# A recalibrated list scheduler in a two-layer diffusion backbone: other latencies, other engine preferences, the first modulation loaded ahead

## The chip, the cores and the metric

The kernel runs on one core of a Trainium2 chip. The metric is the device time of one execution in microseconds (us); lower is better. TensorE (PE) multiplies matrices, VectorE (DVE), ScalarE (ACT) and GpSimd (POOL) work element by element, and SyncE (SP) issues the loads and stores. Each of the five runs its own instructions strictly in the order in which they were issued, and waits on semaphores for what the others produce.

## What is computed

A latent stream `x` of 512 tokens with 1024 features passes two layers, each a modulated RMSNorm, a mixer, a gate and a gated residual; a final RMSNorm follows. Everything is float32. The reference, cut to what matters:

```python
# layer 0
xn = modulate(rms_norm(x, g), shift(c), scale(c))        # adaln: silu(c) @ ada_w + b
cn = modulate(rms_norm(ctx, g), shift(c_ctx), scale(c_ctx))
h = xn @ w_in                                            # conv input, q, k, v and the gate
u = a_val * sigmoid(a_gate); u = depthwise_conv(u, 31 taps)
a = silu(layer_norm(u))
att = latent_window_attention(rope(q), rope(k), v, kc, vc, sink)   # blocks of 128, window and 256 context keys
y = (concat([a, att]) * silu(h_gate)) @ w_out
x = x + gt * y
# layer 1
h = modulate(rms_norm(x, g1), sh1, sc1) @ od_w_in         # bg, cg, u, z of 2048 each
x = x + gt1 * ((bg * depthwise_conv(cg * u, 3 taps)) * silu(z)) @ od_w_out
return rms_norm(x, final_g)
```

## The kernel before, in words

The host only rearranges the weights. In the kernel, activations lie with features on partitions, 1024 features in eight tiles of 128 x 512 (`k` = 0 to 7). Each float32 operand is split into a rounded high part (suffix `h`, a copy on ACT) and the rest (suffix `l`, a subtraction); a product is three matmuls, hi x hi, hi x lo and lo x hi (`mm3`).

The program records every operation first (class `Plan`; so all rows have line L481, the place where they are issued) and then orders them: `schedule()` plays the five engines with modelled durations (`cost`), a delay between producer and consumer (`LAG`, `HOP`), a model of the load queue, and priorities. A priority is the place in the program plus a bias that a stream carries (`CONV_BIAS`, `GATE_BIAS`, `LN_BIAS`, `OUT_BIAS` and so on). An operation issued through `F` may run on DVE or POOL: it goes where the model ends it first, after `SHY` has added a handicap in nanoseconds to DVE. `LOOK` and `HELD` say how long an engine may be kept free for a more urgent operation and for the turn of an SBUF port that the model lets DVE and POOL take one after the other. What comes out is one fixed order for each engine.

The stages, with the names that rows show. *Start:* `cols`, `ccol`, `crow` (the conditioning), four token tiles `xt` and two context tiles `ct` are loaded; `crow` goes through a matmul and Silu into `silb`; ACT squares the tokens (`xt0q`), their factor `xt0r` comes from POOL, and DVE scales them. *Modulation of tile k* (`modulation`): weights `adas` give the shift (`pmod`, 8 small products with `ccol`), `ada` times `silb` gives the scales `mod`, both end in `mab`. *Projection:* for each k the tokens are turned (`tp`, in one PSUM bank "cv"), modulated by ACT, split into `xh` and `xl`, and multiplied with `ws` for keys, queries and values (`pk`, `pq`, `sv`; `pkc` for the context). *Attention:* four groups of four blocks; scores `s`, their maximum by a reduction on DVE (two in each block), `p` by Exp on ACT with the negative maximum `nm`, transposes `pt`, split into `th` and `tl`, product `po`. Between them stand the products of the convolution's input (`ag`, `av`), later queries (`pq`) and gates (`pg`). The 31-tap convolution of a channel tile runs as a chain of `cv` instructions on DVE (30, after one on ACT), for tiles 0 and 5 as `pr`/`cp` on ACT and POOL. *Gate and LayerNorm:* eight gate products `pgc` with weights `wgc0` to `wgc7`, and over the eight convolved tiles `u` a LayerNorm: `lnsum` adds up seven tiles, `lnm` is their mean by a matmul, `u<-u,lnmean` subtracts it, `lnsq` adds the squares, `lnq` sums them by matmuls, `lnb` and `lnr` spread mean and factor. *Output:* `pya` with `woa` (the attention's half, needs no LayerNorm), then `pya`/`pyb` with `woc` (the convolution's half, needs `z0` to `z7`). *Between the layers:* `x` plus the gated output in two halves of columns (hf), squares `sq`, their sum `st`, `xm`, `yh`, `yl`. The modulation of layer 1 comes from `as` and `ac` products, eight each, through one buffer "ad". *Layer 1:* products `pcg`, `pu`, `pbg`, `pz` for 16 tiles, a mixer on DVE, then `f`.

## Time and profile before

| | us |
|---|---|
| median of 3 runs (lowest, highest) | 1005.02 (1001.16, 1007.85) |
| the profiled execution | 1005.3 |
| its span | 1003.5 |
| PE busy in the span | 970.0 (97%) |
| DVE busy | 605.8 (60%) |
| ACT busy | 487.7 (49%) |
| POOL busy | 409.3 (41%) |

The profile's span begins with the first instruction and ends with the last; some 1.8 us lie around it. The share of busy time is a mean over stages with different limits. A row of a timeline gives a start, a duration and, in brackets, how long the engine stood idle before it and what ended that idle time. The profile also lists the clock that was granted to TensorE (1.00 is 2.4 GHz, half of it 1.2 GHz).

### The profile page before, as it was taken

Reading aid. Unit: us, or ns where it says so; the run is one execution under the profiler, and the core shown is the slowest. Engines: PE = TensorE matmul, PEld = TensorE weight load, DVE = VectorE, ACT = ScalarE, POOL = GpSimd, SP = SyncE. Lnnn points to the kernel's source line nnn. Section 1 sums busy time; section 2 is a strip of 40 time slices with the busy share of each in tenths; the row PEclk is TensorE's granted clock in tenths of the full one; section 3 lists DMA queues with packets and bytes.
Section 4 is the critical chain, followed back from the end, with each engine's and each line's share of the span. In section 5 each row is a group of like instructions: output and inputs, shape, how many; then the busy total and the mean of one; then the engine's idle time right before and its main releaser. Section 6 shows DMA issues by size and latency. Waiting matters only on the chain.

```text
span 1003.5 us, 13484 instructions
## 1 busy us (share of the span) xinstructions
PE 970.0 (97%) x4996; PEld 806.4 (80%) x4996; DVE 605.8 (60%) x982; ACT 487.7 (49%) x923; POOL 409.3 (41%) x368
## 2 busy tenths in 40 slices
PE   8989999999999999699999999999999999999997
PEld 5988777778778778578898988888888888888886
DVE  4635887987888889767316666544444444542443
ACT  6647779776887864434425323223323333222332
POOL 4615787666878868878866200000000000000111
PEclk9989999999999999989999999999999999999999
DMA  8632111112121516243154235332332322322222
GB/s 328 212 141 64 64 43 42 43 42 93 56 84 58 175 63 220 96 156 118 63 189 165 89 126 193 101 105 88 101 104 86 105 89 101 105 84 91 98 85 85
DMA packets 31750, 109.11 MB, mean 109 GB/s; under 512 B 3650, under 2 KB 3778, under 8 KB 31684
## 3 DMA queue, kind: packets, MB, share of 16 engines
q1 hardware_dynamic: 31684, 108.25, 32.2%
q8 instruction: 39, 0.64, 0.3%
q14 instruction: 27, 0.22, 0.1%
HBM read 106.14 MB, written 2.10 MB: 108 GB/s over the span
## 4 chain that ended last, share of the span: by engine, by line
PE 77%; DVE 7%; POOL 4%; DMA 4%; ACT 4%; issue 2%; SPq 0%; POOLq 0%; ACTq 0%; DVEq 0%
PE pbg L481 9%; PE pcg L481 9%; PE pz L481 9%; PE pu L481 9%; PE f L481 8%; PE pya L481 6%; PE pq L481 3%; DVE cv L481 3%; PE s L481 3%; PE po L481 3%; PE ag L481 3%; PE pt L481 3%; PE av L481 2%; PE pgc L481 2%; PE sv L481 2%
## 5 line engine op out<-in xcount | busy, mean ns | idle before, releaser
L481 POOL TENSOR_TENSOR x1t<-x1t,fg 128x512 f32<-128x512 f32 x4 | 6.8, 1722 | 392.5 <-ACT fy L481 392.5
L481 DVE SCALAR_TENSOR_TENSOR cv<-u,cols,cv 128x512 f32<-128x512 f32 x180 | 135.4, 752 | 14.6 <-ACT cv L481 10.6
L481 POOL TENSOR_TENSOR cp<-cp,pr 128x512 f32<-128x512 f32 x60 | 78.9, 1315 | 3.6 <-ACT pr L481 1.6
L481 DVE TENSOR_TENSOR tl<-pt,th 128x512 fp32r<-128x512 f32 x72 | 48.1, 689 | 22.6 <-ACT th L481 21.1
L481 PE MATMUL pt<-ident,p 128*128 128x128 f32 x288 | 49.4, 277 | 3.6 <-ACT p L481 3.2
L481 ACT ACTIVATE th<-pt 128x512 fp32r<-128x512 f32 x72 | 41.0, 595 | 20.5 <-PE pt L481 19.6
L481 ACT ACTIVATE p<-s,nm 128x512 f32<-128x512 f32 (+1 forms) x64 | 46.8, 739 | 7.3 <-DVE nm L481 6.9
L481 PEld LDWEIGHTS pt<-ident,p 128*128 128x128 f32 x288 | 35.7, 140 | 17.1 <-ACT p L481 9.9
L481 DVE TENSOR_REDUCE s<-s 128x2 f32<-128x1024 f32 (+1 forms) x32 | 43.5, 1359 | 4.1 <-PE s L481 3.7
L481 ACT ACTIVATE pr<-u,cols 128x512 f32<-128x512 f32 x60 | 41.4, 718 | 5.5 <-POOL cp L481 3.9
L481 PE MATMUL po<-th,vv 128*128 128x512 f32 x72 | 31.0, 431 | 0.6 <-ACT th L481 0.5
L481 PE MATMUL po<-tl,vv 128*128 128x512 f32 x72 | 31.0, 430 | 0.2 <-DVE tl L481 0.2
L481 DVE TENSOR_TENSOR ya<-ya,sz 128x512 f32<-128x512 f32 x16 | 11.1, 692 | 31.0 <-ACT sz L481 30.9
L481 DVE SCALAR_TENSOR_TENSOR ac<-ac,silc 128x1024 f32<-128x1024 f32 x6 | 9.6, 1594 | 29.2 <-DMA ac<-in_ada_dram 29.2
L481 ACT ACTIVATE sz<-pz 128x512 f32<-128x512 f32 x16 | 9.6, 597 | 34.7 <-PE pz L481 34.7
L481 DVE SCALAR_TENSOR_TENSOR ya<-cu,cols,ya 128x512 f32<-128x512 f32 x32 | 24.1, 752 | 1.1
L481 ACT ACTIVATE tp<-tp,mab 128x512 f32<-128x512 f32 (+1 forms) x16 | 10.2, 640 | 24.6 <-PE tp L481 17.5
L481 PEld LDWEIGHTS pmod<-ccol,adas 128*128 128x128 f32 x128 | 19.5, 231 | 2.9 <-DMA adas<-in_adas_dram 2.3
L481 PE MATMUL pmod<-ccol,adas 128*128 128x2 f32 x128 | 19.2, 271 | 1.0 <-DMA adas<-in_adas_dram 0.7
L481 PEld LDWEIGHTS po<-th,vv 128*128 128x128 f32 x72 | 13.5, 188 | 6.4 <-ACT th L481 5.5
L481 DVE TENSOR_TENSOR ya<-pbg,ya 128x512 f32<-128x512 f32 x16 | 11.1, 691 | 12.4 <-PE pbg L481 12.3
L481 PEld LDWEIGHTS po<-tl,vv 128*128 128x128 f32 x72 | 13.7, 190 | 5.1 <-DVE tl L481 3.3
(1671 smaller groups left out, 3444.4 us busy)
## 6 DMA issues: line engine op xcount, KB each, us to landing
wicg<-in_wi_dram SPq DMA_DIRECT2D x16, 512.0 KB, 3.4
wiu<-in_wi_dram SPq DMA_DIRECT2D x16, 512.0 KB, 3.3
wibg<-in_wi_dram SPq DMA_DIRECT2D x16, 512.0 KB, 3.3
wiz<-in_wi_dram SPq DMA_DIRECT2D x16, 512.0 KB, 3.4
wf<-in_wo_dram SPq DMA_DIRECT2D x16, 512.0 KB, 3.4
adas<-in_adas_dram SPq DMA_DIRECT2D x8, 512.0 KB, 3.9
ada<-in_ada_dram SPq DMA_DIRECT2D x8, 512.0 KB, 4.4
wb<-in_wi_dram SPq DMA_DIRECT2D x8, 512.0 KB, 3.4
```

What stands on the lines that cost most here:

```text
L481: op.a = op.fn(*a, **k)
```

## The change

The constants of the scheduler change, and with them the order on every engine. In the model, PE is reached 160 ns after its producer and not 56; a load costs SP 450 ns and not 60, no more than eight loads are under way, the first lands after 2000 ns at 413 bytes per ns; a `pow` on POOL costs 370 ns more; Tanh no longer counts as needing the exponential's table. DVE's handicap for operations that may go to either engine rises from 5617 to 6104 ns in general, but is 500 ns in the gate stage, −367 ns in the LayerNorm (a preference for DVE) and −195 ns from the output projection on.

Three edits are in the program itself. The modulation of tile 0 is recorded ahead of the tokens with a bias of −22000, its scale `ada0` loaded first, and `adas` is loaded in two halves of 256 KB into the "p" buffers rather than in one of 512 KB into "B"; `ws0` follows the tokens. A one-element Exp after the last Silu of the start takes the place of a one-element Tanh. In `normed`, one DVE instruction adds both halves and EPS, so that POOL does only the power. The diff:

```diff
 ADA_POOL = ((1, 5), (1, 3, 5, 7), (1, 5))
-SHY = {'DVE': 5617.0}
+SHY = {'DVE': 6104.0}
+GATE_SHY = {'DVE': 500.0}
+LN_SHY = {'DVE': -367.0}
+WO_SHY = {'DVE': -195.0}
 HI_SHY = {'POOL': 1000.0}
-NORM_SHY = {'ACT': -1220.0}
+NORM_SHY = {'ACT': -876.0}
 HI_TAGS = ()
-LOOK = 0.83
+LOOK = 0.41
 SOON = 0
-HELD = 0
-SWAP_COST = 900.14
-K1_BIAS = 4.11
-Q_BIAS = (-0.62, 1.16, 3.66, 4.5)
+HELD = 45.49
+SWAP_COST = 857.84
+K1_BIAS = 2.65
+Q_BIAS = (-0.32, 1.16, 3.66, 4.5)
 FILL_BIAS = (0.69, -2.96, 1, 3.86, 4.15, 4, 5, 8.19)
-GATE_BIAS = (4.5, 7.18, 10.43, 10, 11.57)
-ADA_BIAS = 14.35
-OUT_BIAS = 15.23
-LN_BIAS = 10.29
+GATE_BIAS = (4.5, 7.18, 11.26, 10, 13.71)
+ADA_BIAS = 13.32
+OUT_BIAS = 15.84
+LN_BIAS = 9.52
 LN_LAST = 7
...
 W0_F = (2, 3)
-CONV_BIAS = 16.5
-CONVP_BIAS = 31.25
+CONV_BIAS = 14.95
+CONVP_BIAS = 26.21
 SWAP = [(i + 16) % 32 for i in range(32)]
...
 LAG = {"PE": 165, "ACT": 100, "DVE": 84, "POOL": 56, "SP": 0}
-HOP = {"PE": 56, "ACT": 35, "DVE": 35, "POOL": 78, "SP": 60}
-ACT_SET = {AF.Exp: "exp", AF.Tanh: "exp", AF.Silu: "silu"}
+HOP = {"PE": 160, "ACT": 35, "DVE": 35, "POOL": 78, "SP": 60}
+ACT_SET = {AF.Exp: "exp", AF.Silu: "silu"}
...
             op.nbytes = v.n * 4 * (v.p1 - v.p0)
-            op.dur = 60
+            op.dur = 450
             return
...
             op.dur = 147 + 2.105 * n if m == "tensor_tensor" else 38 + 1.5 * n
+            if k.get("op") == ALU.pow:
+                op.dur += 370
...
         used, turn, waiting, alloc = {}, {}, {}, set()
-        dma_free, aset, port = 0.0, None, 0.0
+        dma_free, aset, port, landed = 0.0, None, 0.0, []
...
             for e in ENGINES:
+                if e == "SP" and len(landed) >= 8:
+                    free[e] = max(free[e], landed[-8])
                 if avail[e]:
...
             if e == "SP":
-                dma_free = max(dma_free, now + 1000) + op.nbytes / 360.0
-                op.end = dma_free + 1000 - 60
+                dma_free = max(dma_free, now + 2000) + op.nbytes / 413.0
+                op.end = dma_free
+                landed.append(dma_free)
             order.append(op)
...
             A_.activation(sil[e][:, n * 512:(n + 1) * 512], pb, AF.Silu)
+    silb_last = plan.ops[-1]
     plan.bias = -30000
...
     plan.bias = 0
+    ccol_last = plan.ops[-1]
...
-    A_.activation(dm, dm, AF.Tanh)
+    with plan.after(ccol_last, silb_last):
+        A_.activation(dm, dm, AF.Exp)
...
             A_.activation(sq, t[:, n * 512:(n + 1) * 512], AF.Square, scale=1.0 / 32, accum_out=r[:, n:n + 1])
-        V.tensor_tensor(r[:, 0:1], r[:, 0:1], r[:, 1:2], op=ALU.add)
-        rstd(r[:, 0:1], r[:, 0:1])
+        V.tensor_scalar(r[:, 0:1], r[:, 0:1], r[:, 1:2], EPS, op0=ALU.add, op1=ALU.add)
+        G.tensor_tensor(r[:, 0:1], r[:, 0:1], mhalf[:, 0:1], op=ALU.pow)
         V.tensor_scalar(t, t, r[:, 0:1], None, op0=ALU.mult)
...
         return ts
-
-    xt = tokens(x_d, [("A", 4)] * NT, "xt")
...
-    def modulation(k):
-
-
-        shift, scale = load_ada(adas_d[k], f"adas{k}"), load_ada(ada0_d[KT + k], f"ada{k}")
+    def load_ws(k):
         wr = new((P, 640), F32, "wr", f"ws{k}", 3)
...
         ws.append(wr)
+
+    def modulation(k):
+
+
+        scale = load_ada(ada0_d[KT + k], f"ada{k}")
+        shift = [new((P, 640), F32, "p", f"adas{k}_{n}", 8)[:, 0:512] for n in range(2)]
+        for n in range(2):
+            SP.dma_start(out=shift[n], in_=adas_d[k, :, n * 512:(n + 1) * 512])
+        if k:
+            load_ws(k)
         o = pmod[:, 2 * k:2 * k + 2]
         for j in range(KT):
-            T.matmul(o, lhsT=shift[:, j * P:(j + 1) * P], rhs=ccol[:, j], start=j == 0, stop=j == KT - 1)
+            T.matmul(o, lhsT=shift[j // 4][:, j % 4 * P:(j % 4 + 1) * P], rhs=ccol[:, j], start=j == 0, stop=j == KT - 1)
         V.tensor_scalar(mab[:, k, 1], o, col("sh0", k), None, op0=ALU.add)
...
+    plan.bias = -22000
     modulation(0)
+    plan.bias = 0
+    xt = tokens(x_d, [("A", 4)] * NT, "xt")
+    load_ws(0)
     W = [latent_tile(0)]
...
     sgc = []
+    plan.shy = GATE_SHY
     with plan.after(last), plan.stream("gate", GATE_BIAS[4]):
...
     plan.bias, plan.name = 1e5 * LN_BIAS, "ln"
+    plan.shy = LN_SHY
     first = [j for j in range(KT) if j != LN_LAST]
...
     plan.bias, plan.name = 1e5 * OUT_BIAS, ""
+    plan.shy = WO_SHY
     x1 = pairs("A", "x1_")
```

Three places where the order differs. The first is ACT in the start, up to the modulated tile `tp0_0` and its split `xh0`, the first operand of the projection; before:

```order
L481 ACTIVATE wsh0_223<-ws0_148 128x512
L481 ACTIVATE wsv0_229<-ws0_148 128x128
L481 ACTIVATE mab_217<-mod_221,scg_109,cols_76 128x1
L481 ACTIVATE tp0_0_225<-tp0_0_225,mab_217 128x512
L481 ACTIVATE xh0_252<-tp0_0_225 128x512
L481 ACTIVATE ct0q_256,ct0r_257<-ct0_155 128x512
```

and of the change, from the first table load on:

```order
L489 ACT_TABLE_LOAD
L489 ACTIVATE dm_114<-dm_114 128x1
L489 ACTIVATE ct0q_258,ct0r_259<-ct0_174 128x512 x2
L489 ACTIVATE ct1q_265,ct1r_266<-ct1_189 128x512
L489 ACTIVATE ada0_116,mod_179<-ada0_116 128x1024
L489 ACTIVATE mab_193<-mod_179,scg_109,cols_76 128x1
L489 ACTIVATE ct1q_265,ct1r_266<-ct1_189 128x512
L489 ACTIVATE wsh1_291<-ws1_169 128x512
L489 ACTIVATE wsv2_294<-ws2_225 128x128
L489 ACTIVATE mab_193<-mod_179,scg_109,cols_76 128x1
L489 ACTIVATE tp0_0_248<-tp0_0_248,mab_193 128x512
L489 ACTIVATE xh0_313<-tp0_0_248 128x512
```

The table load with its one-element Exp on `dm`, the squares of both `ct` tiles, the copy of `ada0` and the weights `wsh1` and `wsv2` now stand ahead of `tp0_0`; before, the squares of `ct` came behind `xh0`.

The second is PE at `lnm`, the mean of the LayerNorm, between the gate products `pgc`; before:

```order
L481 MATMUL pgc2_4278<-xl4_574,wgc2h1_4232 128x512
L481 MATMUL pgc2_4278<-xh4_568,wgc2l1_4250 128x512
L481 MATMUL lnm_4309<-lnsum_2056,ones_78 128x512
L481 LDWEIGHTS ident_84
L481 MATMUL lnq_4312<-ones_78,ident_84 128x256
L481 LDWEIGHTS ident_84
L481 MATMUL lnq_4312<-ones_78,ident_84 128x256
L481 MATMUL pgc2_4278<-xh5_658,wgc2h1_4232 128x512
```

and of the change:

```order
L489 MATMUL pgc0_4208<-xh2_450,wgc0l0_4133 128x512
L489 MATMUL pgc0_4208<-xh3_528,wgc0h0_4118 128x512
L489 MATMUL lnm_4226<-lnsum_2119,ones_78 128x512
L489 LDWEIGHTS ident_84
L489 MATMUL lnq_4230<-ones_78,ident_84 128x256
L489 LDWEIGHTS ident_84
L489 MATMUL lnq_4230<-ones_78,ident_84 128x256
L489 MATMUL pgc0_4208<-xl3_540,wgc0h0_4118 128x512
```

It moved from behind 63 of the 192 gate matmuls (within tile 2) to behind 10 of them (within tile 0). The rest of the gate products of the change run in the order of their tiles, where before `wgc5` and `wgc6` began ahead of the second half of `wgc4`.

The third is who carries the LayerNorm's sums, around the end of convolution tile 6 and the start of tile 7. Before, on POOL, ahead of the weight's low half `wgc4l1` (second half of tile 4):

```order
L481 TENSOR_TENSOR u1_1356<-u1_1356,lnmean_4317 128x512
L481 TENSOR_TENSOR u2_2538<-u2_2538,lnmean_4317 128x512
L481 TENSOR_TENSOR lnsq3_4411<-lnsq3_4411,lnsq2_4377 128x512
L481 TENSOR_TENSOR lnsq4_4417<-lnsq4_4417,lnsq3_4411 128x512
L481 TENSOR_TENSOR lnsq5_4421<-lnsq5_4421,lnsq4_4417 128x512
L481 TENSOR_TENSOR lnsq6_4425<-lnsq6_4425,lnsq5_4421 128x512
L481 TENSOR_TENSOR wgc4l1_4434<-wgc4_4217,wgc4h1_4349 128x512
L481 TENSOR_TENSOR wgc5l1_4446<-wgc5_4262,wgc5h1_4390 128x512
```

and of the change, on DVE, from the last taps of tile 6 (`cv6`) on:

```order
L489 SCALAR_TENSOR_TENSOR cv6_3442<-u3_3362,cols_76,cv6_3442 128x512 x2
L489 SCALAR_TENSOR_TENSOR sg3_1_4200<-sg3_1_4200,pg3_1_4150 128x512
L489 TENSOR_TENSOR sg3_1_4200<-sg3_1_4200,pi3_1_4198 128x512
L489 TENSOR_TENSOR lnsum_2119<-lnsum_2119,u3_3362 128x512
L489 SCALAR_TENSOR_TENSOR cv7_4216<-u3_3362,cols_76,cv7_4216 128x512
L489 TENSOR_TENSOR wgc1l1_4228<-wgc1_4093,wgc1h1_4205 128x512
L489 SCALAR_TENSOR_TENSOR cv7_4216<-u3_3362,cols_76,cv7_4216 128x512
L489 TENSOR_TENSOR u0_1018<-u0_1018,lnmean_4233 128x512
L489 SCALAR_TENSOR_TENSOR cv7_4216<-u3_3362,cols_76,cv7_4216 128x512
L489 TENSOR_TENSOR u0_1018<-u0_1018,lnmean_4233 128x512
L489 SCALAR_TENSOR_TENSOR cv7_4216<-u3_3362,cols_76,cv7_4216 128x512
L489 TENSOR_TENSOR u1_1367<-u1_1367,lnmean_4233 128x512
```

All six `lnsum` and six `lnsq` additions moved from POOL to DVE, one between two taps of `cv7`, and the low halves of the `wgc` weights no longer stand behind them on POOL. Over the whole program DVE gets 55 instructions more and POOL 61 fewer, PE and ACT keep their counts; SP issues 232 loads and stores, not 224.

## Rows read from the trace of the kernel before

**Rows 1.** Windows: stretch and length, busy time (instructions) per engine, granted clock, DMA share.

```profile
core 0: us, PE busy (x) PEld busy (x) DVE busy (x) ACT busy (x) POOL busy (x), PEclk, DMA share, GB/s
0.00:20.00 20.00, 16.48 (x50) 10.71 (x50) 7.98 (x24) 11.26 (x28) 9.29 (x23) 1.00 0.91 337
20.00:85.00 65.00, 61.81 (x394) 57.24 (x395) 34.68 (x64) 34.10 (x80) 27.02 (x25) 0.89 0.48 167
100.00:376.00 276.00, 271.01 (x1472) 212.77 (x1472) 230.40 (x354) 212.08 (x410) 207.83 (x193) 1.00 0.21 69
400.00:425.00 25.00, 18.53 (x72) 13.81 (x70) 18.20 (x25) 11.90 (x21) 20.21 (x15) 0.93 0.34 112
425.00:455.00 30.00, 25.98 (x121) 21.70 (x122) 19.99 (x31) 10.05 (x18) 22.85 (x17) 0.89 0.47 158
545.00:562.00 17.00, 13.29 (x93) 11.99 (x92) 13.04 (x29) 12.26 (x29) 12.31 (x15) 0.90 0.28 94
```

**Rows 2.** Timeline of ACT, first 25 us: start, duration, operation, [idle before, releaser].

```profile
14.15 0.63 ACT L481 ACTIVATE wsh<-ws 128x512 fp32r<-128x512 f32 x1
...
19.23 0.75 ACT L481 ACTIVATE tp<-tp,mab 128x512 f32<-128x512 f32 x1 [2.53 <-PE tp L481]
...
20.50 0.62 ACT L481 ACTIVATE ct0q<-ct 128x512 f32<-128x512 f32 x1
21.02 0.19 ACT L481 ACTIVATION_READ_ACCUMULATOR ct0q<-ct 128x1 f32 x1
```

**Rows 3.** Timeline of PE before its first projection product, same columns.

```profile
15.40 3.41 PE L481 MATMUL pmod<-ccol,adas 128*128 128x2 f32 x16
...
20.66 0.80 PE L481 MATMUL pk<-xh,wsh 128*128 128x512 f32 x1 [1.53 <-ACT xh L481]
```

**Rows 4.** Timelines of ACT, then PE, at the attention's first exponential.

```profile
108.61 1.28 ACT L481 ACT_TABLE_LOAD   x1 [2.79 <-DVE nm L481]
...
110.73 0.33 PE L481 MATMUL pt<-ident,p 128*128 128x128 f32 x1 [1.49 <-ACT p L481]
```

**Rows 5.** Timeline of PE in the gate and LayerNorm stage.

```profile
407.15 1.12 PE L481 MATMUL lnm<-lnsum,ones 128*128 128x512 f32 x2 [3.50 <-POOL lnsum L481]
...
420.26 0.39 PE L481 MATMUL pgc<-xh,wgc4l 128*128 128x512 f32 x1
420.49 0.39 PE L481 MATMUL pgc<-xh,wgc4h 128*128 128x512 f32 x1
...
428.65 0.80 PE L481 MATMUL pgc<-xh,wgc4l 128*128 128x512 f32 x1 [6.62 <-POOL wgc4l L481]
```

**Rows 6.** Timeline of POOL in the same stage.

```profile
421.74 5.63 POOL L481 TENSOR_TENSOR lnsq<-lnsq,lnsq 128x512 f32<-128x512 f32 x4 [2.04 <-ACT lnsq L481]
427.33 1.26 POOL L481 TENSOR_TENSOR wgc4l<-wgc,wgc4h 128x512 fp32r<-128x512 f32 x1
```

**Rows 7.** Timeline of DVE in the same stage.

```profile
444.67 1.39 DVE L481 TENSOR_TENSOR u<-u,lnmean 128x512 f32<-128x512 f32 x1 [2.33 <-ACT u L481]
446.82 2.16 DVE L481 TENSOR_TENSOR lnsq<-lnsq,lnsq 128x512 f32<-128x512 f32 x1 [0.77 <-ACT lnsq L481]
```

**Rows 8.** Lines by form, DVE: operation, shapes, count, busy us, mean ns, idle before.

```profile
L481 DVE SCALAR_TENSOR_TENSOR cv<-u,cols,cv 128x512 f32<-128x512 f32 x180 | 135.4, 752 | 14.6 <-ACT cv L481 10.6
...
L481 DVE TENSOR_TENSOR tl<-pt,th 128x512 fp32r<-128x512 f32 x72 | 48.1, 689 | 22.6 <-ACT th L481 21.1 <-PE po L481 0.5
...
L481 DVE TENSOR_REDUCE s<-s 128x2 f32<-128x1280 f32 x16 | 23.9, 1491 | 1.7 <-PE s L481 1.7
...
L481 DVE TENSOR_TENSOR wf_7l<-wf,wf_7h 128x512 fp32r<-128x512 f32 x4 | 2.7, 687 | 4.1 <-ACT wf_7h L481 4.1
```

**Rows 9.** Timelines of DVE, then PE, between the layers.

```profile
536.83 1.23 DVE L481 SCALAR_TENSOR_TENSOR ac<-ac,silc 128x1024 f32<-128x1024 f32 x1 [1.13 <-DMA ac<-in_ada_dram]
...
538.38 3.22 DVE L481 SCALAR_TENSOR_TENSOR x<-pya,gtc,x 128x256 f32<-128x256 f32 x8
...
553.58 0.39 PE L481 MATMUL pcg<-yh,wicg0h 128*128 128x256 f32 x1 [1.72 <-ACT yh L481]
```

## The prediction

> **What bounds the kernel now.** I read the windows first, since the share of busy time of the whole span says nothing about one stage. In layer 1 TensorE has no gap: a window there reads 434.00 us busy of 434.00, and the change does not touch that code. So the time can only move where TensorE idles, or where it runs at a lowered clock. [rows 1] shows these places. From 20 to 85 us, the projection over eight k-tiles, TensorE idles 65.00 − 61.81 = 3.2 us; the mean granted clock is 0.89, and with levels of 2.4 and 1.2 GHz that costs 0.11 × 65 = 7.2 us. The attention, 100 to 376 us, idles 5.0 us at a full clock. The gate and LayerNorm stage idles 6.5 us with 0.07 × 25 = 1.8 us of clock (400 to 425 us), and 4.0 us with 0.11 × 30 = 3.3 us of clock (425 to 455 us): 15.6 us together. Between the layers, 545 to 562 us, 3.7 us idle and 0.10 × 17 = 1.7 us of clock. Before 20.66 us TensorE has no projection work at all. These losses of some 36 us, and the start, are all that a new order can win.
>
> Then the timelines of the engines that TensorE waits for. In the gate stage it stands 3.50 us for the LayerNorm's sum and 6.62 us for `wgc4l` [rows 5]. Both come from GpSimd, which runs in order: `wgc4l` stood there behind four `lnsq` additions of 5.63 us, which themselves waited 2.04 us for ScalarE [rows 6]. Nothing is slow there; the weight's low half stands behind work that nobody needs yet. Between the layers VectorE reaches the first `x<-pya` at 538.38 us, only after the last `ac` product, which waited for its load [rows 9].
>
> **Start: later by about 6 us, then denser; −2.6 us.** The loads of `ada0`, `adas0` (1 MB) now precede the four `xt` tiles. In the first 20 us the queue moved 337 GB/s at a DMA share of 0.91 [rows 1], so 1 MB is 3.1 us; about 1 us of it falls where nothing was in flight yet, leaving 2 us by which `xt` is late. Ahead of the first `tp` ScalarE now also has a table load (1.28 us, [rows 4]), four halves of `ct` (0.62 + 0.19 us each, overlapping to about 0.75, so 3.0), a 1024-wide copy of `ada0` (two of the 0.63 us for 512, so 1.25) and a second `wsh` (0.63) [rows 2]: 6.2 us. Against that stand the 2.53 us for which ScalarE idled before `tp`, and some smaller waits, perhaps 3.9 us in all. So the first product, at 20.66 us before [rows 3], comes 2 + 6.2 − 3.9 = 4.3 to 8.2 us later; I take 6, because the chain through GpSimd's `ada` product lies in front too.
>
> What comes back: four k-tiles' modulation products instead of two precede the first product. Sixteen of them took 3.41 us at the slow start [rows 3], so two tiles' worth at full clock is about 1.7 us off the path. With all modulation weights in early, the stage's 10.4 us of idle and lowered clock can shrink; I keep 3.5 us for the first tiles, which still feed one PSUM bank through ScalarE and VectorE, and take back 6.9. Sum: +6 − 1.7 − 6.9 = −2.6. Bounds: 8.2 late with nothing back, +8.2; 4.3 late with everything back, −7.8.
>
> The Trainium skill, "DMA: Bandwidth & Descriptors", Bandwidth, asks for 1 MiB or more per DMA, which speaks against cutting `adas` into halves of 256 KB. No row of before times two such halves against one; if each half cost the rate of a short transfer the stage would lie nearer to its upper bound.
>
> **The table load: −1.3 us.** Before the first exponential ScalarE loads its table for 1.28 us, and TensorE's `pt` behind it waits 1.49 us [rows 4]. The load now stands in the start, where it is counted above. Bounds: 0 (another chain was as late) and −1.5.
>
> **Gate and LayerNorm: −9.5 us.** The old stalls of 3.50 and 6.62 us and the clock after them go, since `lnsum` and `lnsq` leave GpSimd and the low halves of `wgc0` to `wgc7` stand nearly alone there. In place of it VectorE carries the sums, and TensorE asks earlier: `lnm` stands behind 10 gate matmuls, not 63. At 0.23 us apart [rows 5] these 53 matmuls are 12 us. VectorE reaches the last `lnsum` with 9 convolution taps fewer after its last `tl` (13, not 22; 9 × 0.752 = 6.8 us, [rows 8]), and the sum itself no longer queues on GpSimd, so I expect 0 to 1.5 us of wait at `lnm`.
>
> The next meeting is the last `lnq`. From `lnm` TensorE needs 182 + 12 matmuls, 44.6 us, and about 1 us of `lnq`. VectorE has 30 taps (22.6 us), six `u<-u,lnmean` at 1.2 (7.2; a row of it reads 1.39), five `lnsq` additions, four `wgc` halves at 1.0 (4), two `as` at 1.4 (2.8), two `woa` halves (2), 2.3 us of wait for ScalarE, one more `u` and `lnsq` (2.5). The price of an addition from two SBUF tiles is uncertain: 0.687 us for `wf_7l`, where GpSimd is idle [rows 8], and 2.16 us for the one `lnsq` beside a busy GpSimd [rows 7]. I take 1.25, since GpSimd keeps fewer of them, which makes 6.3 and a sum of 49.7. So TensorE waits about 4 us at `lnq`, and some 2 us of lowered clock follow, as followed the old stalls. 15.6 − 6 = 9.6, taken as −9.5. Bounds: all additions at 0.69 shorten VectorE by some 7 us and leave only the old small waits, −14; at 2.16 us they lengthen it by about 10 us, and nothing is left, 0. Behind `lnq` the output projection `woa` covers what is late on VectorE.
>
> **Between the layers: −3.5 us.** In the new order VectorE has finished all `ac`, `mod` and `mab` before the first `x`, and the first `st` products stand between the last `pyb` ones, where TensorE is busy. Of the 5.4 us lost here about 2 remain for `yh` (1.72 us of wait, [rows 9]). Bounds: −5.4, and 0 if the `ac` loads, which follow one another through one buffer, come no earlier while TensorE does.
>
> **Attention: 0, ±5 us.** VectorE has 19 instructions more between the first and the last `tl`: eleven taps (8.3 us), five `lnsum` (3.5 us at 0.69), one `ag`, one `as`, one small. That is some 14.5 us into 276 − 230.4 = 45.6 us of idle [rows 1]. Its cover is this idle time; TensorE itself is busy for 271.01 us, so 5 is all that can be won.
>
> **Sum.** The profiled execution took 1005.3 us (span 1003.5 and 1.8 around it), 0.3 above the median 1005.02. 1005.3 − 2.6 − 1.3 − 9.5 − 3.5 = 988.4.
>
> **The rivals.**
> *Start not recovered.* The first product is 6 us late and each k-tile stays paced by the chain through its one PSUM bank (`tp` waits for TensorE before ScalarE, 2.53 us, [rows 2]): 1005.3 + 6 − 1.3 − 9.5 − 3.5 = 997.0. Against it: the loads ran at 167 GB/s in this stage, half the rate of the start [rows 1], so weights that are asked for earlier come earlier, and less stands between two tiles.
>
> *VectorE takes GpSimd's place in the LayerNorm.* The additions cost 2.16 us each, VectorE is 10 us later at `lnq`, and the whole stage gains nothing: 1005.3 − 2.6 − 1.3 − 3.5 = 997.9. The 2.16 us row speaks for it [rows 7]; against it, GpSimd's own list there is shorter, so fewer pairs meet. The Trainium skill gives the rule behind such a pair in "SBUF — State Buffer", Who interferes with whom: a VectorE instruction with two SBUF inputs and a GpSimd one that reads SBUF exclude one another for their whole length, so moving work between these two need not help. By that rule the trace's 2.16 against 0.687 us is this exclusion, and the case is this rival.
>
> *VectorE holds up the attention (slower).* It runs in order, so a tap set ahead of a score reduction delays `p`, `pt` and `po` by 0.752 us. There are two times 16 such reductions (one of the two rows in [rows 8]); one more tap ahead of each costs 32 × 0.752 = 24.1 us, 988.4 + 24.1 = 1012.5. It decides from 16.9 / 24.1 = 0.7 taps per reduction on. For it: VectorE is 83% busy there already and gets 14.5 us more. Against it: `tl` waits 21.1 us for ScalarE's `th`, so VectorE has been the one that waits [rows 8], and only eleven taps are added for 32 reductions.
>
> *Nothing moves.* The chip waits for other things than the model thinks, each stall reappears one step on: about 1005.
>
> **How the numbers follow.** The forecast's case 0.64 (with its own bounds 978 to 995), start not recovered 0.10, LayerNorm not gained 0.10, attention held up 0.11, nothing moves 0.05. A measurement here tells about 1% from no change, 995 to 1015. Faster by more: 0.64 and a part of the second and third cases, whose 997 lies close to the bound, 0.68. Slower by more: 0.10, most of the attention case and any two bad bounds together. Within: 0.22. Range: 974, where the attention's 5 us and the lower bounds of two terms come in, to 1004, which takes in the second and third cases and half of the last; outside are the attention case and the other half, about 0.14.
>
> **What would show it.** First `pk` at 25 to 29 us, yet the last `sv` of the projection 2 to 3 us earlier than before, and a granted clock above 0.89 in 20 to 85 us. No wait over 2 us for a `wgc` low half; waits of TensorE at `lnm` under 1.5 and at `lnq` about 4 us. `lnsq` on VectorE near 1.25 us. The first hf0 `x<-pya` without a wait on an `ac` load. The forecast is wrong if TensorE's idle time in the attention exceeds some 10 us, or the LayerNorm stage loses 15 us again under another name.

## The result, and the profile after

The changed kernel takes 993.11 us in the median of 4 runs (992.49 to 994.97); the kernel before takes 1004.98 beside it (4 runs, 1001.16 to 1007.85). The ratio is 0.9887, with a 95% interval of 0.9851 to 0.9923: 1.1% faster, 11.9 us where 16.6 to 16.9 were forecast. The profiled execution took 993.6 us, its span 991.8. The kernel before ran 52 times more beside the experiments, on three chips, with a median of 1002.6 us; the changed kernel was not run again there. Against that median the gain is 9.5 us.

The windows of the changed kernel, same columns as [rows 1]: stretch and length, busy time and instructions of each engine, granted clock, DMA share, GB/s.

```profile
0.00:20.00 20.00, 15.28 (x44) 9.44 (x44) 5.98 (x22) 11.05 (x29) 5.39 (x17) 1.00 0.93 348
20.00:85.00 65.00, 62.17 (x398) 57.40 (x398) 39.65 (x65) 35.57 (x81) 33.25 (x24) 0.97 0.47 164
100.00:376.00 276.00, 266.28 (x1455) 211.06 (x1454) 242.99 (x370) 210.41 (x408) 202.79 (x188) 1.00 0.22 73
400.00:425.00 25.00, 25.00 (x112) 20.68 (x112) 23.36 (x29) 14.20 (x24) 18.03 (x12) 1.00 0.50 167
425.00:455.00 30.00, 29.11 (x145) 24.29 (x144) 24.27 (x41) 11.42 (x20) 14.38 (x11) 1.00 0.48 158
545.00:562.00 17.00, 16.83 (x141) 16.46 (x140) 14.43 (x41) 7.75 (x18) 1.59 (x2) 1.00 0.38 125
```

TensorE's idle time and lowered clock in the gate and LayerNorm stage went from 15.6 us to 0.9 (400 to 455 us); 545 to 562 us is nearly full. In the attention the idle time rose from 4.99 to 9.72 us. Since windows cut at fixed times, the stages are better measured between the starts of TensorE's first products: up to each cut the traces of both kernels show the same number of TensorE instructions (432, then 1616, then 436).

| us, profiled executions | before | after | difference | forecast |
|---|---|---|---|---|
| start and projection, up to the first `ag` | 82.28 | 83.24 | +0.96 | −2.6 |
| attention, first `ag` to first `pgc` | 306.83 | 310.38 | +3.55 | −1.3 (table) and 0 |
| gate, LayerNorm, `woa`, first `pgc` to first `woc` | 108.93 | 96.40 | −12.53 | −9.5 |
| first `woc` to TensorE's end | 498.41 | 494.83 | −3.58 | −3.5 |

So the two large gains came as forecast or better, and the smaller gains at the front became losses. In the third row TensorE now waits for the LayerNorm twice, and for no weight (timeline of PE: start, duration, operation, [idle before, releaser]).

```profile
396.98 1.10 PE L489 MATMUL lnm<-lnsum,ones 128*128 128x512 f32 x2 [0.84 <-DVE lnsum L489]
...
442.13 1.05 PE L489 MATMUL lnq<-ones,u 128*128 128x1 f32 x8 [0.89 <-DVE u L489]
```

Against [rows 5]: 3.50 us at `lnm` became 0.84, the 6.62 us for `wgc4l` are gone, and what came in their place at `lnq` is 0.89.

### The profile page after: what moved, and what is told of

Same layout as the page of the kernel before. It is cut to its first block, busy times and chain, and to the rows that moved or that the text cites. A ratio compares the mean times of both kernels' runs of the same rounds, so it can differ in the third digit from the quotient of the medians.

```text
span 991.8 us, 13473 instructions
## 1 busy us (share of the span) xinstructions
PE 964.2 (97%) x4996; PEld 804.2 (81%) x4996; DVE 645.8 (65%) x1037; ACT 488.7 (49%) x923; POOL 350.5 (35%) x307
## 4 chain that ended last, share of the span: by engine, by line
PE 77%; DVE 6%; ACT 5%; POOL 4%; DMA 4%; issue 2%; POOLq 0%; SPq 0%; DVEq 0%; ACTq 0%
PE f L489 9%; PE pbg L489 9%; PE pz L489 9%; PE pcg L489 9%; PE pu L489 9%; PE pya L489 5%; PE av L489 3%; PE pq L489 3%; PE s L489 3%; PE pg L489 3%; PE ag L489 2%; PE pt L489 2%; PE po L489 2%; PE pgc L489 2%; POOL cp L489 2%
## 5 line engine op out<-in xcount | busy, mean ns | idle before, releaser
L489 PE MATMUL pt<-ident,p 128*128 128x128 f32 x288 | 53.5, 276 | 4.4 <-ACT p L489 2.9
L489 PEld LDWEIGHTS pmod<-ccol,adas 128*128 128x128 f32 x128 | 21.9, 261 | 3.4 <-ACT xt0q L489 1.5
L489 PE MATMUL pmod<-ccol,adas 128*128 128x2 f32 x128 | 21.8, 294 | 0.0
L489 ACT ACTIVATE tp<-tp,mab 128x512 f32<-128x512 f32 (+1 forms) x16 | 10.3, 641 | 22.1 <-PE tp L489 16.9
L489 DVE SCALAR_TENSOR_TENSOR silb<-ada,silb 128x1024 f32<-128x1024 f32 x8 | 13.2, 1645 | 6.7 <-DMA xt<-in_x_dram 6.7
```

The source lines that it names most:

```text
L489: op.a = op.fn(*a, **k)
```

## The experiments

Two questions were open: what turned the start's and the attention's forecast around, and what in the change wins the 12.5 us. "Frozen" means that the operations keep the changed kernel's order on every engine but for the edit shown. Each kernel was compared with the kernel before on the same chip; that one's median was 1002.3 to 1002.7 us in each of the three sets of runs (995.95 to 1006.4). Stage times below are cut as in the table.

**1. Is the start held by the work put ahead of `tp0`?** In the frozen order, only what `xh0` needs (and the next tile's weights) stays ahead of it:

```diff
...
+    late = [o for o in order[dm:at] if not stays(o) and not weight(o)]
...
+    order = head + turn[:act] + second + turn[act:] + [order[at], low] + late + between + third + tail
```

> The changed kernel with its order kept everywhere but in the start: ahead of the first modulated tile stands only what that tile needs. The table load with its Exp, the squares of ct, the copy of ada0, wsh1 and wsv2 (ScalarE), the ada1 product (VectorE) and the ada0 product (GpSimd) come behind xh0 and xl0, the transposes of the first tile ahead of the modulation products of tile 2. Theory 'queue ahead': the first pk, at 28.70 us in the changed kernel, comes at 22 to 24, and the projection (end at 83.2) ends 3 to 5 us earlier, so the whole takes 988 to 990. Rival 'paced by the tiles': the projection is set by loads and by the chain through one PSUM bank, so the first pk comes earlier but the end stays within 1 us, the whole at 992 to 994. A third way: the second tile waits for what was put back, and the end is 1 to 3 us later.

Measured: 995.58 us, ratio 0.9941 [0.9921, 0.9962]; first `pk` at 28.48 us, first `ag` at 86.37. The first product did not move. ScalarE now idles where its squares and copies stood (timelines of ACT, DVE and PE of this kernel, each in a fence):

```profile
25.52 0.75 ACT L489 ACTIVATE tp<-tp,mab 128x512 f32<-128x512 f32 x1 [5.67 <-PE tp L489]
```

```profile
22.07 2.82 DVE L489 TENSOR_SCALAR xt<-xt,xt3r 128x1024 f32<-128x1024 f32 x1 [0.45 <-POOL xt3r L489]
```

```profile
24.94 0.47 PE L489 MATMUL tp<-ident,xt 128*128 128x128 f32 x1 [2.79 <-DVE xt L489]
25.21 3.41 PE L489 MATMUL pmod<-ccol,adas 128*128 128x2 f32 x16
28.48 0.77 PE L489 MATMUL pk<-xh,wsh 128*128 128x512 f32 x1
```

The scaling of the fourth token tile takes 2.82 us (0.75 for the first) beside GpSimd's `ada` product, the last transpose waits for it, and 16 `pmod` products stand behind that. This last transpose stands 1.1 us earlier than in the changed kernel, but 16 `pmod` products follow it where 12 did there, so the edit gave back part of what it won. In the changed kernel itself ScalarE is ready when the last transpose arrives (PE, then ACT):

```profile
26.00 0.47 PE L489 MATMUL tp<-ident,xt 128*128 128x128 f32 x1 [0.99 <-DVE xt L489]
```

```profile
26.59 0.72 ACT L489 ACTIVATE tp<-tp,mab 128x512 f32<-128x512 f32 x1
```

ScalarE's queue, from which I had worked out the six microseconds, was not what set the first product.

**2. The same start with the needed work first on every engine.** Frozen order again, the whole start ranked by what `xh0` needs:

```diff
...
+    head = sorted(order[:at], key=rank)
+    order = head + order[at:]
...
```

> The changed kernel with its order kept from the first context tile on; in the start every engine first does what the first modulated tile needs, then what the second needs, then the rest. Against the run s_front, three more things are put back: VectorE no longer waits for a modulation product of TensorE ahead of the tokens' scaling (3.22 us idle there), GpSimd does the four powers ahead of the weights' low halves, and only the 8 modulation products of tile 0 stand ahead of the first projection product, not 24. Theory 'these three set the start': the first pk comes at 20 to 22 us, 7 us earlier than in the changed kernel. For the end of the projection, 83.1 us in the changed kernel: if a tile's pace of 6.4 us is kept, 77 to 80 and a total of 987 to 990; if the projection is paced by loads and by the granted clock, 82 to 85 as in s_old, whose first pk came at 19.7, and 992 to 995.

Measured: 994.73 us, 0.9932 [0.9908, 0.9956]; first `pk` at 20.90 us, as early as before, yet the first `ag` at 86.94, 3.7 us later than in the changed kernel. The time comes back at the fifth tile (timeline of DVE, then of PE):

```profile
36.13 1.75 DVE L489 TENSOR_SCALAR ct<-ct,ct1r 128x1024 f32<-128x1024 f32 x1
37.81 0.21 DVE L489 TENSOR_SCALAR mab<-pmod,cols 128x2 f32<-128x2 f32 x1
```

```profile
38.07 2.29 PE L489 MATMUL pmod<-ccol,adas 128*128 128x2 f32 x10 [2.66 <-DVE mab L489]
```

`pmod` is one tile, so TensorE's next `pmod` waits until VectorE has read the last with `mab`; that stood behind the scaling of a context tile. This stretch also ran at a granted clock of 0.89 from 20 to 85 us, 0.97 in the changed kernel. An earlier first product is worth nothing by itself here; that the tiles' modulation paces the stage is read from this wait, and the lower clock stands beside it as a second cause.

**3. The start as before, the rest of the change kept** (tokens first, one load for `adas`, the sum of `normed` as before; the order made anew):

```diff
...
-    plan.bias = -22000
     modulation(0)
-    plan.bias = 0
-    xt = tokens(x_d, [("A", 4)] * NT, "xt")
-    load_ws(0)
```

> The changed kernel with the old program for the start (tokens loaded first, adas in one load of 512 KB, POOL adds EPS), all constants, the latencies and the early Exp as changed; the whole order is made anew from it. Theory 'queue ahead': the first pk comes at about 21 to 24 us as in the kernel before, yet the projection ends within 1 us of the 83.2 of the changed kernel, since late modulation weights cost there what the late first product costs here; the gate and LayerNorm part keeps its gain of 12.5 us: 991 to 994. Rival 'new loads lose': the projection ends 3 us or more earlier than 83.2, total 988 to 990. Rival 'new loads win': it ends 3 us or more later, total 996 or more.

Measured: 993.51 us, 0.9911 [0.9876, 0.9946], not told apart from the changed kernel. In its profiled execution the first `pk` came at 19.75 us and the first `ag` at 86.34. What happened between is the clock. The windows 20 to 85 us of this kernel, of the kernel of experiment 7, and of that of experiment 5:

```profile
20.00:85.00 65.00, 62.30 (x371) 57.81 (x372) 31.11 (x58) 32.35 (x76) 24.27 (x22) 0.82 0.46 159
```

```profile
20.00:85.00 65.00, 60.71 (x414) 55.59 (x415) 38.81 (x66) 38.51 (x89) 30.62 (x28) 1.00 0.47 167
```

```profile
20.00:85.00 65.00, 62.17 (x408) 57.46 (x409) 41.68 (x70) 36.69 (x83) 35.51 (x26) 1.00 0.49 165
```

Experiment 7 has the start of the kernel before, instruction for instruction on every engine; at a clock of 1.00 its first `ag` stands at 77.94 us, against 82.28 at 0.89 [rows 1]. Experiment 5 has the changed start; at 1.00 its first `ag` stands at 82.08, against 83.24 at 0.97. At equal clock, then, the new start is 3.0 to 4.1 us slower (80.96 us, of experiment 6, being its best), by one execution of the old start at that clock. The totals don't show it: 993.5 us with the old start against 993.1, and 989.4 (experiment 11) against 990.6 (experiment 5). What it had in its favour is that the eight profiled executions with a start of the new kind (all but experiments 1 and 2) read 0.95 to 1.00, those with one of the old kind 0.82, 0.89, 0.92 and 1.00. That is too few to call it a property of the order.

**4. The exponential's table loaded in the attention again**, frozen order:

```diff
...
+            o.a = (o.a[0], o.a[1], AF.Tanh if o.a[2] == AF.Exp else o.a[2])
```

> The changed kernel with its order kept; only the one-element instruction after the last Silu is a Tanh again, so that the exponential's table is loaded before the first exponential of the attention. If the early load is worth what the trace of before showed (1.3 us), the start loses 1.3 us on ScalarE and the attention gets a wait of about 1.3 us at its first pt: total 992.5 to 994.5, first pk 1.3 us earlier, with no measurable difference. If the start has room for it, the total is 1 us higher (994 to 995). If the attention has room for it, 1 us lower (991.5 to 992.5).

Measured: 991.42 us, 0.9906 [0.988, 0.9933]. ACT, then PE:

```profile
110.51 1.28 ACT L489 ACT_TABLE_LOAD   x1 [2.38 <-DVE nm L489]
```

```profile
112.64 0.33 PE L489 MATMUL pt<-ident,p 128*128 128x128 f32 x1 [0.84 <-ACT p L489]
```

The load is back before the first exponential and TensorE waits 0.84 us; yet the first `pgc` starts at 393.66 us, in the changed kernel at 393.62. The early load is worth nothing that shows.

**5. The attention's five `lnsum` additions back on GpSimd**, frozen order:

```diff
...
+        if name(o) == "lnsum" and o.eng == "DVE":
+            o.eng = "POOL"
...
```

> The changed kernel with its order kept; only the five lnsum additions that stand ahead of the attention's last tl run on GpSimd, in the same places (3.5 us less for VectorE). Theory 'VectorE over-full': the idle time of TensorE between 100 and 376 us, 9.7 us, falls by 1 to 3 us, as moving 11 taps out took it to 7.2. Rival 'single places': only the taps ahead of certain tl matter and the idle time stays within 0.7 us of 9.7. Either way the total is within 3 us of 993.

Measured: 990.55 us, 0.9902 [0.9871, 0.9934]; attention 307.5 us (310.4), TensorE idle 7.24 us (9.72) from 100 to 376 us; experiments 1 and 2, with the additions on VectorE, have 7.66 and 7.35, so the idle time alone shows nothing. TensorE's waits in that stretch (waiting <- releaser: us in total, times, longest), of the changed kernel, then of this one:

```profile
PE pt L489 <- ACT p L489: 2.9, 3, 1.4
PE po L489 <- DVE tl L489: 2.4, 4, 1.0
PE pq L489 <- DVE att L489: 1.6, 1, 1.6
PE po L489 <- ACT th L489: 1.0, 1, 1.0
```

```profile
PE pt L489 <- ACT p L489: 1.8, 2, 1.3
PE pq L489 <- DVE att L489: 1.6, 1, 1.6
PE po L489 <- DVE tl L489: 1.5, 3, 1.0
```

Before, `po` waited 0.2 us for `tl` and none of these waits for `att` was there.

**6. The eleven taps that came into the attention put behind it**, frozen order:

```diff
...
+    moved = [order[i] for i in taps if i < end][-11:]
...
+    order = rest[:at] + moved + rest[at:]
```

> The changed kernel with its order kept, but the last 11 convolution taps of the attention (8.3 us of VectorE) come behind the attention's last tl. TensorE idles 9.7 us between 100 and 376 us in the changed kernel, 5.0 in the one before. Theory 'VectorE over-full': the waits at po and pt for tl late in the attention (1.06, 0.58, 1.00 and 0.86 us after 340 us) fall below 0.5 each and the gate products begin 2 to 3 us earlier than 393.6; the LayerNorm's mean then waits 6 to 9 us, so the total is 996 to 1001. Rival 'order of TensorE': the idle time in the attention stays at 9 to 10 us, the gate products begin within 0.7 us of 393.6.

Measured: 1002.11 us, 0.9989 [0.997, 1.0009]. First `ag` to last `po` takes 295.0 us (297.4 in the changed kernel, 293.4 before), but experiments 1 and 2, which leave the taps where they were, take 295.9 and 295.5: that the attention gets something back is not shown. Then TensorE stands for VectorE (waits of PE, 376 to 500 us):

```profile
PE pi L489 <- DVE sg L489: 3.7, 1, 3.7
PE lnm L489 <- DVE lnsum L489: 3.5, 1, 3.5
```

The clock of 376 to 400 us reads 0.93, of 400 to 425 us 0.86; the gate and LayerNorm stage takes 102.1 us instead of 96.4. The taps cost the attention nothing beyond its spread, and having them done early is what lets VectorE reach the LayerNorm in time.

How sure is the attention's part? Six profiled executions share the changed order there: 310.4, 310.0 (experiment 4), 308.8 (1) and 308.5 us (2) with the additions on VectorE, 307.5 and 308.7 (12) with them on GpSimd. The means differ by 1.3 us and the two sets overlap. In the order of experiment 3 the same move takes the attention from 310.7 to 307.5 us (11). So the additions may cost 1 to 3 us; two sets this small don't prove it.

**7. The three new handicaps alone, in the kernel before:**

```diff
+GATE_SHY = {'DVE': 500.0}
+LN_SHY = {'DVE': -367.0}
+WO_SHY = {'DVE': -195.0}
...
```

> The kernel before with the three handicaps of the change (500, -367 and -195 ns from the gate stage on) and nothing else. Theory 'who carries the sums': the waits for lnsum and wgc4l on GpSimd go, the stage from the first gate product to the first woc falls from 108.9 to 95 to 100 us, the step between the layers by some 3 us, total 988 to 994. Rival 'biases and latencies': the sums on VectorE are late behind its convolution taps, the stage keeps 104 us or more, total 1000 to 1005.

Measured: 1004.84 us, 1.0027 [1.0001, 1.0053], no gain, as the rival had it. Gate and LayerNorm took 105.6 us, 3.3 less than before; `lnm` stands behind 95 gate matmuls. TensorE's waits from 376 to 500 us:

```profile
PE pya L484 <- POOL woa7l L484: 2.4, 1, 2.4
PE pgc L484 <- DVE wgc5l L484: 1.7, 1, 1.7
PE lnm L484 <- DVE lnsum L484: 1.6, 1, 1.6
```

Behind the first `woc` it lost 6.9 us against before, part of it at a clock of 0.79 from 545 to 562 us.

**8. The change without them:** one handicap everywhere.

```diff
-GATE_SHY = {'DVE': 500.0}
-LN_SHY = {'DVE': -367.0}
-WO_SHY = {'DVE': -195.0}
+GATE_SHY = SHY
+LN_SHY = SHY
+WO_SHY = SHY
```

> The changed kernel with one handicap of 6104 ns for VectorE in all stages, so that lnsum and lnsq go to GpSimd as before; biases, latencies and the start as changed. Theory 'who carries the sums': gate, LayerNorm and output product by woa, 96.4 us from the first gate product to the first woc in the changed kernel and 108.9 before, take 104 to 110 again, with a wait of 2 us or more for a GpSimd result; total 1000 to 1006. Rival 'biases and latencies': the stage stays at 95 to 99 us, since the earlier LayerNorm and the longer modelled way to TensorE are what moved the stalls: 991 to 996.

Measured: 1020.33 us, 1.0188 [1.0143, 1.0234], slower than before and beyond the 1000 to 1006 expected. All six `lnsum` and six of seven `lnsq` are on GpSimd again, ahead of the gate's first weights (POOL, then PE):

```profile
396.58 3.48 POOL L489 TENSOR_TENSOR lnsq<-lnsq,lnsq 128x512 f32<-128x512 f32 x2
400.02 2.31 POOL L489 TENSOR_TENSOR u<-u,lnmean 128x512 f32<-128x512 f32 x2
402.29 5.30 POOL L489 TENSOR_TENSOR lnsq<-lnsq,lnsq 128x512 f32<-128x512 f32 x4
...
413.51 1.28 POOL L489 TENSOR_TENSOR wgc0l<-wgc,wgc0h 128x512 fp32r<-128x512 f32 x1
```

```profile
414.84 0.79 PE L489 MATMUL pgc<-xh,wgc0l 128*128 128x512 f32 x1 [17.30 <-POOL wgc0l L489]
```

It is the stall of [rows 6] again, 17.30 us instead of 6.62, since the new biases bring the LayerNorm forward: `lnm` starts at 389.74 us, ahead of the first gate product. The stage took 119.8 us. The handicaps move more than the sums: of GpSimd's work during this wait (397.5 to 414.8 us) 7.8 us are `lnsq`, 2.3 `u<-u,lnmean`, and 6.0 products and low halves of `att`, `z` and `as`.

**9. The change with the old biases** (and `LOOK`, `HELD`, `SWAP_COST`, general handicaps); handicaps of the stages, latencies and start kept:

```diff
...
-GATE_BIAS = (4.5, 7.18, 11.26, 10, 13.71)
-ADA_BIAS = 13.32
-OUT_BIAS = 15.84
-LN_BIAS = 9.52
+GATE_BIAS = (4.5, 7.18, 10.43, 10, 11.57)
+ADA_BIAS = 14.35
+OUT_BIAS = 15.23
+LN_BIAS = 10.29
...
-CONV_BIAS = 14.95
-CONVP_BIAS = 26.21
+CONV_BIAS = 16.5
+CONVP_BIAS = 31.25
```

> The changed kernel with the old biases, LOOK, HELD, SWAP_COST and general handicaps, while the three new stage handicaps, the latencies of the model and the new start stay; the order made anew. lnm then stands behind 70 gate matmuls, not 10. Theory one, the biases turn the handicaps into the gain (the handicaps alone on the kernel before gave 3.3 us of that stage's 12.5): the stage from the first pgc to the first woc product takes 102 us or more, and the kernel 998 to 1004. Theory two, the new latencies do (PE reached after 160 ns, loads limited to eight under way): the stage stays at 95 to 99 us and the kernel at 990 to 996.

Measured: 1002.51 us, 1.0015 [0.9988, 1.0042]; the stage 102.7 us, as theory one has it. `lnm` stands behind 93 gate matmuls (not 70, as I had expected) and still waits (PE):

```profile
414.68 2.07 PE L489 MATMUL lnm<-lnsum,ones 128*128 128x512 f32 x2 [3.17 <-DVE lnsum L489]
...
417.21 0.80 PE L489 MATMUL pgc<-xh,wgc3h 128*128 128x512 f32 x1
```

VectorE ends the last `lnsum` at 414.6 us, in the changed kernel at 396.8, though TensorE asks 83 matmuls later. The next output products then wait 3.5 us for `woc1l`. The attention took 307.1 us: with the old biases its loss is gone too, although five `lnsum` stand on VectorE there as well.

**10. The change with TensorE's modelled delay as before:**

```diff
-HOP = {"PE": 160, "ACT": 35, "DVE": 35, "POOL": 78, "SP": 60}
+HOP = {"PE": 56, "ACT": 35, "DVE": 35, "POOL": 78, "SP": 60}
```

> The changed kernel with TensorE's modelled delay behind a producer back at 56 ns (160 in the change), all else as changed; the order made anew, lnm behind 36 gate matmuls. If the attention's loss of 3.5 us comes from the order that the longer delay makes, it goes back to 306 to 308 us from the first ag to the first pgc, with TensorE idle 5 us or less from 100 to 376 us. If it comes from VectorE's added work, which this kernel keeps but for one sum, it stays at 309 to 311 us and 8 to 10 us idle. If the longer delay is what wins the LayerNorm stage, first pgc to first woc lasts 100 us or more, and the kernel 996 or more; if the handicaps and biases win it, 96 to 98 us and the kernel within 991 to 995.

Measured: 998.03 us, 0.9963 [0.9939, 0.9986]; the attention 311.0 us with 8.59 us idle, the stage 98.9 us. So the delay doesn't cause the attention's loss, and is worth some 2.5 us in the LayerNorm stage (98.9 lies between the two expectations), part of it a clock of 0.94 from 425 to 455 us. The largest wait of the attention is for VectorE (in the changed kernel it is `pt`'s for ScalarE's `p`, 2.9 us, before 2.4 for `tl`):

```profile
PE po L489 <- DVE tl L489: 3.5, 5, 1.3
```

**11 and 12. Combinations.** Experiment 3 with the additions of experiment 5, and experiments 4 and 5 together:

```diff
...
+        if name(o) == "lnsum" and o.eng == "DVE":
+            o.eng = "POOL"
...
```

> The changed kernel with the start as it was before (tokens first, one 512 KB load for each shift), the order made anew by the changed constants, and the attention's five lnsum additions put back on GpSimd in the otherwise frozen order. If the start's costs and VectorE's load add up independently: the run with the old start alone took 993.5 against 991 to 993 of the changed kernel, and the five additions brought 2 to 3 us of the attention, so about 991. If the old start's long stretch at the low clock (20.5 us in its profiled run) does not come again, which costs some 10 us at half speed less what the queue absorbs, 985 to 988, with the first gate product pgc earlier than 389 us. If the sums on GpSimd meet other VectorE work in this order and cost a wait at lnm of over 2 us, 993 to 996.

> The changed kernel's order with the five attention lnsum additions on GpSimd and the one-element Exp of the start as Tanh again, so that the exponential's table is loaded in the attention. The theory that the attention is held up by VectorE and that the early table load is worth nothing expects the same as with the additions alone: 989 to 991.5, the first gate product within 1 us of 389.6. If the early load is worth the 1.3 us of the sum once VectorE is relieved, it comes 1 to 1.5 us later: 991 to 992.5, with pt behind the load waiting 1.3 us or more.

Measured: 989.36 us, 0.9872 [0.983, 0.9914], and 993.45 us, 0.9896 [0.9845, 0.9947] (987.03 to 994.51 in 4 runs). The intervals of the changed kernel, of experiments 4 and 5 and of both combinations overlap; none is shown to beat the change. In the first, after waits of 0.9 us at `lnm` and 1.0 at `lnq`, the clock from 425 to 455 us reads 0.89 and the stage takes 99.8 us; the changed kernel and six others, with much the same waits there and a clock of 1.00, take 96.0 to 96.5.

## Why the prediction was right, and where not

That the change is faster and where most of it comes from was right. 988.4 was 4.7 us below the median and 5.2 below the profiled execution. By the table, start and attention together came out 8.4 us worse than forecast and the gate stage 3.0 better, so that the total came this near is in part luck. The sum also started from 1005.3 us, a slow execution of the kernel before (median 1002.6 in the 52 later ones).

*Gate and LayerNorm, −9.5 forecast, −12.5 measured.* The step that failed is the 4 us at the last `lnq` and the 2 us of clock behind it. TensorE's side of that sum held: 442.13 − 0.89 − 396.98 = 44.3 us against 44.6 + 1. VectorE's 49.7 us were 44. Its lines from 398 to 442 us (count, busy us, mean ns, idle before):

```profile
L489 DVE SCALAR_TENSOR_TENSOR cv<-u,cols,cv 128x512 f32<-128x512 f32 x29 | 21.7, 750 | 0.5
L489 DVE TENSOR_TENSOR u<-u,lnmean 128x512 f32<-128x512 f32 x7 | 7.4, 1063 | 0.3 <-ACT u L489 0.3
L489 DVE TENSOR_TENSOR lnsq<-lnsq,lnsq 128x512 f32<-128x512 f32 x6 | 6.8, 1139 | 1.0 <-ACT lnsq L489 1.0
```

The prices were right: 1.14 us for an `lnsq` where I took 1.25. But the last `lnsq` (1.40 us) is not needed for the first `lnq`, which sums `u`. And I added durations as if they stood end to end: the 53 instructions of this window add up to 44.8 us while VectorE was busy for 41.6, since one starts before the one ahead has ended (two taps last from 429.54 to 431.09 us, the next instruction starts at 430.99). With one tap fewer (0.75) that is 49.7 − 1.4 − 3.2 − 0.75 = 44.4. The 2 us of clock didn't come either: it stayed at 1.00 behind the waits of 0.84 and 0.89 us, while behind the 3.17 us of experiment 9 a gate product took 0.80 us (0.39 at full clock); experiment 11, though, lost clock behind waits of 0.9 and 1.0. That the stage needs the handicaps is shown by experiment 8; that they need the biases is shown by 7 and 9: 105.6 us with the handicaps alone, 102.7 with the new latencies and start beside them, 96.4 with the biases as well. I had put the whole gain down to the sums leaving GpSimd. As much of it hangs on work moved ahead, so that VectorE has time for them: with eleven taps put back (6) the stage takes 102.1 us. Which of the operations that the handicaps move matters most was not tested one by one; it isn't the first five `lnsum`, since with these back on GpSimd (5) the stage keeps its 96.3 us.

*Between the layers, −3.5 forecast, −3.6 measured.* VectorE reached the first `x<-pya` at 527.62 us with all `ac` done, and TensorE starts `pcg` at 541.94 without a wait ([rows 9]: 553.58 with 1.72). DVE, then PE, of the changed kernel:

```profile
527.62 0.87 DVE L489 SCALAR_TENSOR_TENSOR x<-pya,gtc,x 128x256 f32<-128x256 f32 x2
```

```profile
534.25 0.61 PE L489 MATMUL st<-ones,sq 128*128 128x1 f32 x4 [1.36 <-DVE sq L489]
...
541.94 0.36 PE L489 MATMUL pcg<-yh,wicg0h 128*128 128x256 f32 x1
```
What remains is one wait of 1.36 us, at `st` for VectorE's `sq`, not at `yh`. The cut of this term is rough: 16 of the transposes `xt` moved behind the first `pcg`, so it was taken to TensorE's end. The executions that keep the changed order there lie at 492.3 to 495.5 us, the one of before at 498.4; without the handicaps (8) or the biases (9) it is 499.1 and 499.9, one execution each, so this gain, too, seems to need both.

*Start, −2.6 forecast, +0.96 measured.* The first `pk` came at 28.70 us, inside the 25 to 29 named; being 8.0 us late and not 6, it lay at the upper bound of that step. The reason that carried the number was wrong: experiment 1 took ScalarE's work away and the first product stayed. The chain through GpSimd's `ada` product, named beside it without a price, is what the rows show. Of the delay 7.1 us came back, not 8.6. The 1.7 us for two tiles' modulation products was a misreading: the 16 rows of [rows 3] are one tile's (the trace has 128 for eight tiles), so two tiles are 6.8 us there and, as an estimate, half of it at full clock, 3.4. So 2.0 of the term's 3.6 us are the later first product and 1.5 the smaller return. The step that failed there is the 7.2 us of lowered clock, which I read from one execution as a property of the order and let the new order win back: the same start, instruction for instruction, ran at 1.00 in experiment 7 and was 4.3 us shorter. At equal clock, by that one execution, the change makes the start slower. Of its signs, the granted clock above 0.89 came, the last `sv` 2 to 3 us earlier did not (83.12 against 82.16).

*Table load, −1.3 forecast.* Nothing, by experiment 4. TensorE's 1.49 us in [rows 4] were a wait, but without the load the attention ended no earlier (393.62 against 393.66 us with it). It fits my bound of 0, that another chain was as late; which one, no run shows.

*Attention, 0 ± 5 forecast, +3.55 measured with the table's nothing in it.* The six executions of the changed order there, additions on VectorE or on GpSimd, lie 0.7 to 3.6 us above the one of before. If VectorE is the cause, this is the rival "VectorE holds up the attention" in a small size; TensorE's idle time of 9.72 us stayed just under the "some 10" at which the forecast was to count as wrong. VectorE's busy time rose by 12.6 us, not 14.5, in a stage where it idled 45.6; I argued that the idle time covers it. The lines show how much of that idle time was usable: `tl`'s waits for `th` fell from 21.1 [rows 8] to 9.4 us in all, and waits of TensorE for `tl` and `att` appeared. The five additions also cost more than 0.69 each, one of them 2.68 us (100 to 376 us):

```profile
L489 DVE TENSOR_TENSOR lnsum<-lnsum,u 128x512 f32<-128x512 f32 x4 | 5.3, 1326 | 0.7 <-ACT u L489 0.7
```

The waits and experiments 5 and 11 point to VectorE, and 10 speaks against the modelled delay. But 9 has the five additions on VectorE and almost no loss (307.1 against 306.8), 6 takes eleven taps away and shows no return, and executions of one order differ by 2 us. So what in the new order costs the attention its time stays open.

*The rivals.* "VectorE takes GpSimd's place" didn't come, and the row of 2.16 us on which it stood was one bad meeting and not the mean, which is 1.18 over seven. "Start not recovered" was half right, +0.96 and not +6.

## What to carry to other kernels

When an engine that runs in order carries work that nobody needs yet ahead of work that somebody does, moving that work to another engine pays only together with making room there: here the handicaps alone won 3.3 us of the stage, with the biases that do other work earlier, and the longer modelled delay, 12.5. A lowered clock seen in one execution is not yet a loss of that order; look for it in a second execution before it goes into a sum. And idle time of an engine inside a chain of short waits is no proof that added work is covered: here 12.6 us more work in 45.6 us of idle time went with an attention up to 3.6 us longer.

## What the runs showed of the hardware

The start shows how VectorE and GpSimd hold each other up. Timelines of DVE, then of POOL, in the changed kernel:

```profile
15.34 0.75 DVE L489 TENSOR_SCALAR xt<-xt,xt0r 128x1024 f32<-128x1024 f32 x1
...
17.85 1.21 DVE L489 SCALAR_TENSOR_TENSOR silb<-ada,silb 128x1024 f32<-128x1024 f32 x1
...
19.50 1.75 DVE L489 TENSOR_SCALAR xt<-xt,xt2r 128x1024 f32<-128x1024 f32 x1 [0.31 <-POOL xt2r L489]
...
21.30 3.25 DVE L489 SCALAR_TENSOR_TENSOR ada<-ada,silb 128x1024 f32<-128x1024 f32 x1
...
32.41 1.22 DVE L489 SCALAR_TENSOR_TENSOR ada<-ada,silb 128x1024 f32<-128x1024 f32 x1
```

```profile
16.28 0.55 POOL L489 TENSOR_TENSOR xt1r<-xt1r,mhalf 128x1 f32<-128x1 f32 x1 [3.67 <-DVE xt1r L489]
...
18.01 1.46 POOL L489 TENSOR_TENSOR xt2r<-xt2r,mhalf 128x1 f32<-128x1 f32 x1 [0.75 <-DVE xt2r L489]
19.44 1.26 POOL L489 TENSOR_TENSOR wsl<-ws,wsh 128x512 fp32r<-128x512 f32 x1
20.66 2.81 POOL L489 TENSOR_TENSOR ada<-ada,silb 128x1024 f32<-128x1024 f32 x1
23.43 1.53 POOL L489 TENSOR_TENSOR xt3r<-xt3r,mhalf 128x1 f32<-128x1 f32 x1
```

VectorE's `ada` product takes 1.22 us alone and 3.25 here: GpSimd's ended at 20.66 + 2.81 = 23.47, VectorE's at 21.30 + 3.25 = 24.55, about its own length later. The scaling of a tile, one input from SBUF, took 1.75 us behind `wsl` (0.75 alone). Even GpSimd's power of one element per partition went from 0.55 to 1.46 us, while VectorE's product with `silb` ran (17.85 to 19.06). The Trainium skill states in "SBUF — State Buffer", Who interferes with whom, that whoever comes first has the shared pair for the whole instruction and the other stands still; these rows agree, for a single element too. What I had not expected is that it strikes at the start: the fourth tile's power (23.43) stands behind GpSimd's `ada`, VectorE's scaling behind that power, and the last transpose ahead of the first product behind the scaling.

The other is the spread of the clock over executions of the same instructions: 0.89 and 1.00 from 20 to 85 us for the old start, worth 4.3 us to the first `ag`, and 0.97 and 1.00 for the new one. Over the whole program the kernel before took 995.95 us at a mean granted clock of 0.993 and 1006.4 (twice) at 0.985 and 0.987, among its 52 later executions.
